# All fourteen later heads' values by seven products, and output product 2 in the attention's last period

## The chip, the core and the metric

The kernel runs on one core of one Trainium2 chip. The metric is the device time of one execution in microseconds (us). Five engines work side by side, each through its own list of instructions in order: PE (TensorE, the matmuls), DVE (VectorE), ACT (ScalarE), POOL (GpSimd) and SP (SyncE, which here issues the transfers).

## The reference, cut to what matters

One block of a streaming encoder on a 512 x 2048 sequence, in float32:

```
h    = rmsnorm(x)
proj = h @ w_in                    # q, k, v of 8 + 8 heads of 128 columns, and 8 forget gates
o_sb  = stick_breaking(qa, ka, va) # 8 heads
o_fox = softmax with a decay by the gates (qf, kf, vf)  # 8 heads
x = x + concat(headnorm(o_sb), headnorm(o_fox)) @ w_out
x = x + relu(rmsnorm(x) @ w_up)**2 @ w_down
y = rmsnorm(x)
```

## The kernel before, in words

**Products in three parts.** Every matrix product is made of pairs: a float32 operand is cast to fp32r (the high part, on ACT) and the rest is the low part (a subtraction, on DVE). `mm3` (L76) multiplies high by high, high by low and low by high into one PSUM bank, so a tile of weights costs a load, a cast, a low part and matmuls in threes.

**Seven products for eight.** The larger products go by Winograd's form of Strassen's scheme: the operands are cut into 2 x 2 quadrants and seven products p = 1 to 7 of quadrants or of their sums replace eight. The sums are made on DVE.

**Stages.** (1) Values (V) of the first two heads and the gates, plain. (2) V of twelve heads in two groups of six by the seven-product scheme: each product is 48 matmuls with 384 columns (`NV`), into one of three PSUM banks x, y and z (two of PSUM's eight rooms each). Group 2 runs its products in the order 2, 1, 5, 6, 4, 7, 3 in banks x, y, z, y, x, y, z. At a product's end `saved` (ACT) and `added` (DVE, L566 to L569) scale the bank's rows into a tile, and SP stores it as `vd`. (3) The attention: sixteen heads in periods of 26.05 us, in which PE makes the next head's q and k (`accq`, 96 matmuls with 512 columns), the scores `s` of one head and the output `o` of another. The pool `accb` for half of the `accq` and for `accv` takes over rooms of the V stage. (4) The last period has no next head; PE fills it with `last_values`: V of the last two heads, plain, 192 matmuls with 256 columns into `accv`, and `take_last_values` splits them. (5) The output projection by seven products (banks `accoa`, `accob`, `accoc`), product 2 first for both halves (db) of the columns; the last two heads' outputs `o` and `oq` and their norms are made in between: `square`, `square_low` (L951: the low part of the squares, in `n` for the head before the last and in `pl` for the last), `norm_sums` (L956 and L957: two matmuls with a matrix of ones) and `norm_2`. (6) MLP up and down by seven products.

**What sets the order.** Up to the end of the attention the order within each engine is written out by hand: `plan.at(time, job)` sorts jobs by a planned time. What comes after it (`g_form`, the left operands `g` of the output's products, made from `mixed`; the weights `wo`, `wh`, `wl`) is placed by a scheduler, which may slip it into the list between the jobs of the plan. An instruction waits until what it reads is there and what it overwrites has been used, and all behind it on its engine wait with it.

Of the kernel before, what the change touches and what calls it, by code (L numbers as in the profile page):

```python
# [15 lines left out]
P = 128  # L16
# [12 lines left out]
NV = 3 * P  # L29

# [7 lines left out]
def block_kernel(ctx, tc, x, g_attn, w_in, b_f, g_out_sb, g_out_fox, w_out, g_mlp, w_up, w_down, g_final, y):  # L38
# [82 lines left out]
    vd = [dp.tile([P, TB, 2 * P], F32, name="vd0")] + [dp.tile([P, TB, 2 * NV], F32, name=f"vd{i}") for i in (1, 2)]  # L121
# [99 lines left out]
    with ExitStack() as stage:  # L221
# [12 lines left out]
        def vtile(i):  # L234
            return vq[min(i, 1)].tile([P, K8, NV], F32, tag=f"q{i}", name=f"q{i}")
# [160 lines left out]
        def load_rows_of(t_, group, name, a, b=None):  # L396
            s, j = int(name[0]) - 1, int(name[1]) - 1
            c0 = v_columns(order[2 if group == 1 else 8]) + j * NV
            b = a if b is None else b
            sp.dma_start(t_[:, b:b + 2], vrows[s][:, a:a + 2, c0:c0 + NV])  # L400

        def load_quadrant(group, name, i, rows=range(0, K8, 2)):
            if rows[0] == 0:
                quads[group][name] = vtile(i)
            for a in rows:
                load_rows_of(quads[group][name], group, name, a)
# [52 lines left out]
        class Product(Piece):  # L459
            def __init__(self, p, group, a, T, first):  # L460
                self.p, self.a0, self.T, self.group = p, a, T, group
                self.a, self.b, self.first = 2, NV, first
                self.names = {1: ("11",), 2: ("21",), 3: ("22",), 5: ("11", "12", "11"), 6: ("11", "22", "11"),
                              4: ("21", "21", "11"), 7: ("12", "22", "12")}[p]

            def source(self):
                if self.p == 1 and self.group == 1:
                    return early_11[self.a0 // 4][:, self.a0 % 4:self.a0 % 4 + 2]
                return quads[self.group][self.names[0]][:, self.a0:self.a0 + 2]

            def sum(self):
                out, u, v = (quads[self.group][n][:, self.a0:self.a0 + 4] for n in self.names)
                dve.tensor_tensor(out, u, v, op=ALU.subtract)
# [8 lines left out]
            def multiply(self):  # L482
                ps = self.T[0]
                for t in range(2):
                    ts = slice(t * P, (t + 1) * P)
                    for i in range(2):
                        k = self.a0 + i
                        lh, ll = self.left(k)
                        mm3(ps[:, t, :NV], lh[:, ts], ll[:, ts], self.hi[:, i, :], self.lo[:, i, :],
# [8 lines left out]
        STARTS[2] = {p: END + i * TP for i, p in enumerate((2, 1, 5, 6, 4, 7, 3))}  # L498
        TE = TV + END + 7 * TP
# [8 lines left out]
        def product(p, group, T, new=None, leads=(6.4, 4.2, 2.6)):  # L508
# [3 lines left out]
            for n, a in enumerate(range(0, K8, 2)):  # L512
                w = Product(p, group, a, T, new is not None)
                tm = t + TP / 4 * n
# [45 lines left out]
        def saved(name, tile_, T, t0):  # L560
            out = keep[name] = tile_()
            for i in range(2):
                act.mul(out[:, i, :], T[0][:, i, :NV], r1s[0][:, t0 + i:t0 + i + 1])

        def added(name, T, t0, group, j):
            out = keep[name]  # L566
            for i in range(2):
                dve.scalar_tensor_tensor(out[:, i, :], T[0][:, i, :NV], r1s[0][:, t0 + i:t0 + i + 1], out[:, i, :], op0=ALU.mult, op1=ALU.add)
            sp.dma_start(vd[group][:, t0:t0 + 2, j * NV:(j + 1) * NV], out)  # L569
# [4 lines left out]
        def gates_0():  # L574
            t_ = vf.tile([P, K8 * 2 * P], F32, tag="e3", name="gt")
            gate["tri"], gate["one"] = t_[:, :P], t_[:, P:2 * P]
            r_ = vf.tile([P, K8 * 2 * P], F32R, tag="e4", name="gr")
# [1597 lines left out]
```

## Time and profile before

| | |
|---|---|
| median of 3 runs | 2005.12 us (2004.80 to 2005.39) |
| profiled execution, its own time | 2005.12 us |
| its span (first to last instruction) | 2003.4 us |
| PE busy | 1993.2 us, 10288 matmuls |
| DVE busy | 1746.6 us |
| ACT busy | 1201.9 us |
| mean granted TensorE clock | 0.999 |

A row of the timeline gives the start, the duration, the engine, the line, the operation, what it writes and reads and, in brackets, how long the engine had stood idle and who released it. Matmuls overlap, so their pace is the distance from start to start and not the duration.

### The profile page before, as it was taken

The numbers are of one execution on the slowest core, as the hardware profiler recorded it, in microseconds if no ns is written. First come the engines' busy times: TensorE is split into PE (matmuls) and PEld (weight loads), VectorE is DVE, ScalarE is ACT, GpSimd is POOL, SyncE is SP. The second block draws the span as 40 slices with busy tenths as digits, with TensorE's granted clock in tenths as the row PEclk, the third lists the DMA queues.
The fourth block names the chain that finished last, engine by engine and source line by source line (L and its number), as shares of the span: only waits on it lengthen the run. The fifth ranks groups of instructions, "written<-read, shape, count | busy, mean of one in ns | idle before, by whom it ended". The sixth has DMA issues, their size and how long they took to land.

```text
span 2003.4 us, 27063 instructions
## 1 busy us (share of the span) xinstructions
PE 1993.2 (99%) x10288; PEld 1726.3 (86%) x10288; DVE 1746.6 (87%) x1993; ACT 1201.9 (60%) x1643; POOL 64.1 (3%) x73
## 2 busy tenths in 40 slices
PE   9999999999999999999999999999999999999998
PEld 9998888888898889888888888888888888888887
DVE  8886888888877588999999999998798888988896
ACT  7544766787764565767676776766543444444344
POOL 0000011010110000000000000000000000000003
PEclk9999999999999999999999999999999999999999
DMA  7417976777658962666666666666695674674642
GB/s 262 157 65 248 291 232 209 228 223 223 207 177 303 304 227 95 199 202 199 217 183 214 199 207 200 200 209 233 246 334 177 226 277 146 239 263 171 214 163 85
DMA packets 309570, 423.54 MB, mean 211 GB/s; under 512 B 49424, under 2 KB 205376, under 8 KB 302912
## 3 DMA queue, kind: packets, MB, share of 16 engines
q1 hardware_dynamic: 308688, 419.71, 63.6%
q10 hardware_dynamic: 752, 2.11, 0.3%
q8 instruction: 81, 1.33, 0.3%
q14 instruction: 49, 0.40, 0.1%
HBM read 315.45 MB, written 96.49 MB: 206 GB/s over the span
## 4 chain that ended last, share of the span: by engine, by line
PE 98%; DVE 1%; DMA 1%; ACT 0%; issue 0%; SPq 0%; DVEq 0%; ACTq 0%
PE psa L1311 11%; PE accd L78 8%; PE accd L79 8%; PE accd L77 8%; PE accq L77 6%; PE accq L78 6%; PE accq L79 6%; PE psa L1309 6%; PE psc L1311 5%; PE psc L1309 3%; PE psb L1311 3%; PE psb L1309 1%; PE m L78 1%; PE m L77 1%; PE m L79 1%; PE accoc L77 1%
## 5 line engine op out<-in xcount | busy, mean ns | idle before, releaser
L1961 ACT CAST wh<-wd 128x1024 fp32r<-128x1024 f32 x126 | 124.9, 998 | 169.7 <-PE accd L79 59.0
L1847 DVE TENSOR_TENSOR wl<-wu,wh 128x1024 fp32r<-128x1024 f32 x158 | 192.7, 1220 | 12.1 <-ACT wh L1841 11.9
L77 PE MATMUL accq<-hH,wh 128*128 128x512 f32 x512 | 200.3, 391 | 0.0
L78 PE MATMUL accq<-hL,wh 128*128 128x512 f32 x512 | 199.4, 389 | 0.0
L79 PE MATMUL accq<-hH,wl 128*128 128x512 f32 x512 | 199.4, 389 | 0.0
L1841 ACT CAST wh<-wu 128x1024 fp32r<-128x1024 f32 x158 | 167.5, 1060 | 44.1 <-issue 27.9
L1311 PE MATMUL psa<-f,wh 128*128 128x512 f32 x720 | 179.0, 391 | 0.0
L78 PE MATMUL accd<-wl,uf 128*128 128x512 f32 x436 | 169.6, 389 | 0.0
L79 PE MATMUL accd<-wh,uf 128*128 128x512 f32 x436 | 169.6, 389 | 0.0
L77 PE MATMUL accd<-wh,uf 128*128 128x512 f32 x436 | 169.4, 389 | 0.0
L1311 PEld LDWEIGHTS psa<-f,wh 128*128 128x128 f32 x720 | 132.3, 188 | 25.6
L1968 DVE TENSOR_TENSOR wl<-wd,wh 128x1024 fp32r<-128x1024 f32 x126 | 144.0, 1152 | 10.6 <-ACT wh L1961 10.6
L1961 ACT CAST wx<-wd 128x1024 fp32r<-128x1024 f32 (+1 forms) x82 | 80.7, 994 | 106.1 <-PE accd L79 39.6
L1682 DVE TENSOR_TENSOR m<-m,accd 128x1024 f32<-128x1024 f32 x84 | 102.3, 1217 | 45.9 <-PE accd L79 45.9
L79 PEld LDWEIGHTS accq<-hH,wl 128*128 128x128 f32 x512 | 96.1, 188 | 20.3
L77 PEld LDWEIGHTS accq<-hH,wh 128*128 128x128 f32 x512 | 96.2, 188 | 19.0
L78 PEld LDWEIGHTS accq<-hL,wh 128*128 128x128 f32 x512 | 96.2, 188 | 18.9
L77 PE MATMUL accd<-wx,uf 128*128 128x512 f32 x284 | 110.5, 389 | 0.0
L78 PE MATMUL accd<-wx,uf 128*128 128x512 f32 x284 | 110.5, 389 | 0.0
L79 PE MATMUL accd<-wx,uf 128*128 128x512 f32 x284 | 110.5, 389 | 0.0
L1309 PEld LDWEIGHTS psa<-f,wl 128*128 128x128 f32 x720 | 96.0, 191 | 5.4
L1309 PE MATMUL psa<-f,wl 128*128 128x256 f32 x720 | 98.3, 282 | 0.0
(464 smaller groups left out, 5121.3 us busy)
## 6 DMA issues: line engine op xcount, KB each, us to landing
wu<-in_w_up_dram SPq DMA_DIRECT2D x60, 1024.0 KB, 6.3
ufd<-st SPq DMA_DIRECT2D x98, 512.0 KB, 4.0
wd<-in_w_down_dram SPq DMA_DIRECT2D x48, 1024.0 KB, 9.2
uf<-ufd SPq DMA_DIRECT2D x42, 1024.0 KB, 8.1
wraw<-in_w_in_dram SPq DMA_DIRECT2D x68, 512.0 KB, 5.7
wo<-wsums SPq DMA_DIRECT2D x28, 512.0 KB, 5.4
q<-in_w_in_dram SPq DMA_DIRECT2D x32, 384.0 KB, 5.5
wd<-in_w_down_dram SPq DMA_DIRECT2D x16, 768.0 KB, 5.8
```

The lines of the kernel that those rows point to most:

```text
L77: pe.matmul(out, sh, mh, start=first, stop=False, skip_group_check=True)
L78: pe.matmul(out, sh, ml, start=False, stop=False, skip_group_check=True)
L79: return pe.matmul(out, sl, mh, start=False, stop=last, skip_group_check=True)
L1309: ins = pe.matmul(ps[:, 2 * P:], lo[:, a, :], f_parts(p, a)[0], start=False, stop=last, skip_group_check=True)
L1311: ins = pe.matmul(ps, hi[:, a, :], f_both(p, a), start=a == PAIRS[0] and p in (1, 5), stop=last, skip_group_check=True)
L1682: dve.tensor_tensor(M[p][:, :, db, :], M[p][:, :, db, :], ps, op=ALU.add)
L1841: act.copy(rooms[k][0], srcs[k])
L1847: lows[0] = dve.tensor_tensor(lo, srcs.pop(k), hi.bitcast(F32), op=ALU.subtract)
L1961: act.copy(rooms[k + 3][0], srcs[k + 3])
L1968: dve.tensor_tensor(rooms[k + 2][1], srcs.pop(k + 2), rooms[k + 2][0].bitcast(F32), op=ALU.subtract)
```

## The change

Group 2 now holds all eight remaining heads: its products have 512 columns (`NVS[2]`), 48 matmuls each, and the plan gives each of them 10.9 us (`TP2`) for 8.45. The quadrants no longer fit where they were, so tiles are cut in 6 + 2 rows (`load_late`, `quad`), quadrant 21 is loaded twice (`21x`), and sums over a second half are made in two pieces. The order of the products becomes 2, 1, 5, 6, 3, 7, 4, so that the last is product 4 in bank x. The gates' jobs move to 33.0 to 48.5 us in the group. `last_values` and `take_last_values` are gone.

The attention's last period is filled with the output's product 2 (classes `FoxLeft` and `Second`): 96 matmuls with 512 columns into four tiles `acc2`, of which `take_second` adds the results to rows of x. The output stage then begins with product 1; product 4 of the first half follows early, in bank b.

```diff
-        STARTS[2] = {p: END + i * TP for i, p in enumerate((2, 1, 5, 6, 4, 7, 3))}
+        TP2 = 10.9
+        STARTS[2] = {p: END + i * TP2 for i, p in enumerate((2, 1, 5, 6, 3, 7, 4))}
...
             def sum(self):
-                out, u, v = (quads[self.group][n][:, self.a0:self.a0 + 4] for n in self.names)
-                dve.tensor_tensor(out, u, v, op=ALU.subtract)
+                for a, n in ((self.a0, 4),) if self.group == 1 or self.a0 == 0 else ((4, 2), (6, 2)):
+                    out, u, v = (quad(self.group, name, a, n) for name in self.names)
+                    dve.tensor_tensor(out, u, v, op=ALU.subtract)
...
-                pieces = []
-                for a in range(4):
-                    c = v_columns(order[2 * NH - 2])
-                    k0 = 4 * a
-                    w = Piece(w_in[k0 * P:(k0 + 4) * P, c:c + 2 * P].rearrange("(a p) c -> p a c", p=P), 4, 2 * P)
-                    cast, low = ((-9.25, -3.65), (2.3, 3.3), (3.3, 4.5), (10.25, 11.7))[a]
-                    pieces.append(w.plan(plan, t + (-21.0, -15.0, -14.0, -2.0)[a], t + cast, t + low))
+                for i, jobs in ((1, (-9.25, -3.65)), (0, (2.3, 3.3))):
+                    for dt, f in zip(jobs, (fox_left.high, fox_left.low)):
+                        plan.at(t + dt, f, i)
...
+                        for tt in range(2):
+                            plan.at(t + at_unit16(unit), w.multiply, tt)
+                            unit += 1
+                for db in range(2):
+                    plan.at(t + 2.0 + db, load_second_x, db)
+                    for tt in range(2):
+                        plan.at(t + (20.6, 28.5)[db] + 0.75 * tt, take_second, db, tt)
+                t_end = t + at_unit16(15) + 1.37
...
-        for i, dt in ((2 * NH - 2, 1.0), (2 * NH - 1, 3.0)):
+        t = TPER * 2 * NH
+        for i, times in ((2 * NH - 2, (at_unit16(14) - 1.95, 23.1, 24.9, at_unit16(15) + 1.37, 27.4, 29.0)),
+                         (2 * NH - 1, (28.5, 30.5, 32.2, 33.0, 33.5, 34.8))):
             H = heads[i]
-            plan.at(t_end + dt, H.product)
-            plan.at(t_end + dt + 2.0, H.square)
-            plan.at(t_end + dt + 3.7, H.square_low)
-            plan.at(t_end + dt + 4.5, H.norm_sums)
-            plan.at(t_end + dt + 5.0, H.norm_1)
-            plan.at(t_end + dt + 6.3, H.norm_2)
+            for dt, f in zip(times, (H.product, H.square, H.square_low, H.norm_sums, H.norm_1, H.norm_2)):
+                plan.at(t + dt, f)
...
-            g_form(2, (0, 4), (4, 8))
             g_form(1, (0, 4), (4, 6))
             with tc.issue_after(last_heads[2].ins):
                 g_form(4, (0, 4), (4, 8))
                 g_form(5, (0, 4), (4, 6))
...
             with tc.issue_after(last_heads[3].ins):
-                out_piece(2, 0, 2)
+                out_piece(1, 0, 0)
+            with tc.issue_after(last_heads[0].ins):
+                out_piece(1, 0, 2)
+                out_piece(1, 0, 4)
+            begin(1, 0, 0)
+            with tc.issue_after(last_heads[1].ins):
+                for m0 in (0, 2, 4, 6):
+                    ins = out_piece(4, 0, m0)
...
-        for p in G_ORDER:
+        for p in (1, 5, 6, 3, 7, 4)[:6 if db else 5]:
```

In the rows below, what an instruction waits for stands in brackets, by engine or transfer queue.

**From the values to the attention, PE.** Before, the last matmuls of the V stage (bank z) and the first of the attention stand so:

```order
L77 MATMUL vz_1350<-wh_1700,s3_1000 128x384
L78 MATMUL vz_1350<-wl_1701,s3_1000 128x384
L79 MATMUL vz_1350<-wh_1700,s3_1000 128x384
L77 MATMUL accq_1773<-hH0_98,wh_1716 128x512 [waits Activation_49]
L78 MATMUL accq_1773<-hL0_99,wh_1716 128x512
```

and now (bank x) so:

```order
L78 MATMUL vx_1682<-wh_1719,hH3_104 128x512
L79 MATMUL vx_1682<-wl_1720,hH3_104 128x512
L80 MATMUL vx_1682<-wh_1719,hL3_105 128x512
L78 MATMUL accq_1793<-hH0_98,wh_1735 128x512 [waits DVE_49,Activation_49]
L79 MATMUL accq_1793<-hL0_99,wh_1735 128x512
```

The first matmul of the attention waited for ACT's cast alone and now waits for DVE too: its tile lies in rooms of bank x, and DVE's last `added` reads `vx_1682`.

**The same place, SP.** `s0_1525` is the tile of the last `added` before, `s3_1700` that of the change; `wraw` are raw weights of the first head's k (two halves) and of the next head's q. Before:

```order
L569 DMA vd2_89<-s2_1681 128x2x384 [waits DMAHW3_49,DVE_49]
L733 DMA rb_1763<-r1d_91 128x512 [waits DMAHW4_49,DMAHW6_49,DMAHW0_49,PE_49]
L165 DMA wraw_1765<-in_w_in_dram 128x8x128 [waits DMAHW5_49]
L165 DMA wraw_1767<-in_w_in_dram 128x8x128 [waits DMAHW3_49]
L569 DMA vd2_89<-s0_1525 128x2x384 [waits DMAHW7_49,DVE_49]
L165 DMA wraw_1769<-in_w_in_dram 128x8x128 [waits DMAHW1_49,Activation_49]
```

and now:

```order
L590 DMA vd2_89<-gt_1444 128x2x512 [waits DMAHW7_49,DVE_49]
L590 DMA vd2_89<-s3_1700 128x2x512 [waits DMAHW0_49,DVE_49]
L783 DMA rb_1783<-r1d_91 128x512 [waits DMAHW3_49,DMAHW1_49,PE_49]
L166 DMA wraw_1785<-in_w_in_dram 128x8x128 [waits DMAHW2_49]
L166 DMA wraw_1787<-in_w_in_dram 128x8x128
L166 DMA wraw_1789<-in_w_in_dram 128x8x128 [waits DMAHW6_49,DMAHW4_49,Activation_49]
```

The last store stood behind `rb` and two loads of weights; now all three stand behind it.

**The end of the attention, DVE.** `p_last` is the low part of the last head's weights, made when its transposes are done; `pl` in the last row is that head's `square_low`. Before (a row with x2 stands for two instructions):

```order
L913 TENSOR_TENSOR p_last_5466<-pt_5443,p_last_5466 128x1280 [waits DMAHW1_49,Activation_49]
L63 SCALAR_TENSOR_TENSOR vl_5482<-accv_5220,r1v_147,vh_5481 128x256 [waits Activation_49] x2
L63 SCALAR_TENSOR_TENSOR vl_5482<-accv_5221,r1v_147,vh_5481 128x256 [waits Activation_49] x2
L60 TENSOR_TENSOR g4_5576<-mixed_1750,g4_5575 128x1024 x2
L60 TENSOR_TENSOR wx_5687<-wo_5688,wx_5687 128x1024 [waits DMAHW7_49,DMAHW5_49,DMAHW0_49]
L60 TENSOR_TENSOR wl_5705<-wo_5706,wh_5704 128x1024 [waits DMAHW6_49,DMAHW2_49,Activation_49]
L1231 TENSOR_TENSOR mixed_1750<-mixed_1750 128x4x256 [waits DVE_49]
L1231 TENSOR_TENSOR mixed_1750<-mixed_1750 128x2x256 [waits DVE_49]
L951 TENSOR_TENSOR n2_5510<-n1_5509,n2_5510 128x512 [waits Activation_49]
L951 TENSOR_TENSOR pl_5531<-ph_5530,pl_5531 128x512 [waits PE_49,Activation_49]
```

In the change the head before the last has its `n2` ahead of `p_last`, and eight instructions follow `p_last` in these rows:

```order
L962 TENSOR_TENSOR p_last_5462<-pt_5443,p_last_5461 128x1280 [waits Activation_49]
L1167 TENSOR_TENSOR x2_5289<-x2_5289,acc2_5361 128x512 [waits DMAHW2_49]
L61 TENSOR_TENSOR g4_5526<-mixed_1770,g4_5525 128x1024 x2
L61 TENSOR_TENSOR wl_5620<-wo_5621,wh_5619 128x1024 [waits DMAHW6_49,Activation_49]
L1332 TENSOR_TENSOR mixed_1770<-mixed_1770 128x4x256 [waits DVE_49]
L61 TENSOR_TENSOR wl_5638<-wo_5639,wh_5637 128x1024 [waits DMAHW1_49,DMAHW2_49,DMAHW0_49,Activation_49]
L1332 TENSOR_TENSOR mixed_1770<-mixed_1770 128x2x256 [waits DVE_49]
L1015 SCALAR_TENSOR_TENSOR n1_5438<-ssq_5465,ra_5437 128x512 [waits Activation_49]
```

The next ten and the last head's `square_low` follow directly:

```order
L61 TENSOR_TENSOR g5_5520<-mixed_1770,g5_5519 128x1024 [waits PE_49,Activation_49]
L61 TENSOR_TENSOR wl_5656<-wo_5657,wh_5655 128x1024 [waits DMAHW3_49,DMAHW2_49,Activation_49]
L1016 TENSOR_TENSOR n1_5438<-n1_5438,ra_5437 128x512 [waits DVE_49]
L61 TENSOR_TENSOR g5_5520<-mixed_1770,g5_5519 128x512 [waits Activation_49]
L1334 TENSOR_TENSOR mixed_1770<-mixed_1770 128x4x256 [waits DVE_49]
L61 TENSOR_TENSOR wx_5673<-wo_5674,wx_5673 128x1024 [waits DMAHW5_49,DMAHW4_49,Activation_49]
L1017 SCALAR_TENSOR_TENSOR n1_5438<-n1_5438,ra_5437 128x512 [waits DVE_49]
L1334 TENSOR_TENSOR mixed_1770<-mixed_1770 128x2x256 [waits DVE_49]
L1018 SCALAR_TENSOR_TENSOR mixed_1770<-os_5436,g_rest_78,n1_5438 128x512 [waits DVE_49]
L1167 TENSOR_TENSOR x2_5289<-x2_5289,acc2_5362 128x512
L1000 TENSOR_TENSOR pl_5492<-ph_5491,pl_5492 128x512
```

The `g5` lows, the whole `norm_2` of the head before the last and two of the lows of weights stood behind `pl` before, the rows of x (`x2`) not at all in this place; now 18 instructions stand between `p_last` and `pl`, nine of 1024 elements a row and nine of 512.

**The same place, PE.** The matmuls that end with the last head's norm sums, in the change (the 24 `accoa` matmuls between the `oq` product and them end with the first two rows):

```order
L79 MATMUL accoa_5549<-wx_5602,g1_5515 128x512
L80 MATMUL accoa_5549<-wx_5602,g1_5516 128x512
L1005 MATMUL oq_5471<-pl_5492,onesr_114 128x512 [waits Activation_49]
L1006 MATMUL oq_5471<-pl_5492,onesr_114 128x512 [waits DVE_49]
L78 MATMUL accob_5550<-wh_5619,g4_5525 128x512
L79 MATMUL accob_5550<-wl_5620,g4_5525 128x512
```

From the last transpose to the first of the two norm sums PE's list holds 19 matmuls with 512 columns, one sum for the head before the last, the 12 of `oq` and 24 of `accoa`.

More of the change, by code (lines that the diff above doesn't have):

```diff
@@ L672, in block_kernel @@
             X4 = [None]
-            product(2, group, T["x"], "x", (6.9, 4.3, 2.4))
-            plan.at(TV + 13.5 if one else at_[1] + 0.6, saved, "11", lambda: stored(0), T["x"], 0)
+            product(2, group, T["x"], "x", (0, 4.3, 2.4))
+            plan.at(TV + 13.5 if one else at_[1] + 0.6, saved, "11", (lambda: stored(0)) if one else (lambda: third(NVS[2])), T["x"], 0)
             product(1, group, T["y"], "y")
```

258 lines of the change are left out of this document (157 added, 101 removed).

## Prediction

> **What bounds the kernel now.** I read the page's first and fourth parts, then windows around the places that the change touches.
>
> ```profile
> span 2003.4 us, 27063 instructions
> ...
> PE 1993.2 (99%) x10288; PEld 1726.3 (86%) x10288; DVE 1746.6 (87%) x1993; ACT 1201.9 (60%) x1643; POOL 64.1 (3%) x73
> ...
> PE 98%; DVE 1%; DMA 1%; ACT 0%; issue 0%; SPq 0%; DVEq 0%; ACTq 0%
> ```
>
> PE is idle for 10.2 us of 2003.4 and the chain of waits is 98% PE. So the time moves in two ways: by fewer matmul columns, and by every wait that PE newly takes. The windows (V group 2, the start of the attention, its last period, the output) show how little slack for a gain there is:
>
> ```profile
> core 0: us, PE busy (x) PEld busy (x) DVE busy (x) ACT busy (x) POOL busy (x), PEclk, DMA share, GB/s
> 117.00:165.00 48.00, 48.00 (x280) 48.00 (x279) 38.08 (x46) 22.54 (x35) 0.68 (x4) 1.00 0.14 45
> 165.00:190.00 25.00, 25.00 (x115) 20.89 (x114) 14.49 (x20) 8.36 (x11) 1.80 (x2) 1.00 0.94 315
> 560.00:600.00 40.00, 40.00 (x287) 37.88 (x286) 28.90 (x34) 28.64 (x31) 3.77 (x6) 1.00 0.55 176
> 600.00:646.00 46.00, 46.00 (x209) 38.19 (x208) 37.61 (x48) 21.23 (x36) 0.00 (x0) 1.00 0.85 297
> 646.00:650.00 4.00, 3.22 (x13) 2.11 (x12) 2.38 (x2) 2.02 (x3) 0.00 (x0) 1.00 1.03 375
> ```
>
> PE is busy for the whole of the first four windows: both places where the change cuts in, the seam from the values to the attention and the attention's end, have no PE wait today. Only the output stage has one, near 647.
>
> **Matmuls.** Matmuls overlap, so their price is the distance between starts.
>
> ```profile
> 156.76 0.33 PE L77 MATMUL vz<-wh,s 128*128 128x384 f32 x1
> ...
> 165.08 0.39 PE L77 MATMUL accq<-hH,wh 128*128 128x512 f32 x1
> ...
> 563.50 0.28 PE L77 MATMUL accv<-wh,hH 128*128 128x256 f32 x1
> 563.61 0.28 PE L78 MATMUL accv<-wl,hH 128*128 128x256 f32 x1
> 563.73 0.28 PE L79 MATMUL accv<-wh,hL 128*128 128x256 f32 x1
> ...
> 605.15 0.39 PE L77 MATMUL accob<-wx,g 128*128 128x512 f32 x1
> ...
> 616.03 0.39 PE L77 MATMUL accoc<-wx,g 128*128 128x512 f32 x1
> ```
>
> ```profile
> L77 PE MATMUL accv<-wh,hH x64: 277/283/364, 563.5 to 591.8; 128*128 128x256 f32 x64
> ```
>
> A V product's 48 matmuls of 384 columns take 165.08 - 156.76 = 8.32 us, 0.1733 each. A product's half in the output, 48 of 512 columns, takes 616.03 - 605.15 = 10.88 us, 0.2267 each. 256 columns take 0.12. The change drops 3 x 64 = 192 of 256 columns (-23.0 us) and widens 7 x 48 = 336 matmuls from 384 to 512 columns, 336 x 0.0534 = +17.9 us. Output product 2's 96 matmuls are moved, not added. Sum: **-5.1 us**.
>
> **The seam.** The first `accq` now waits for the last `added`, because bank x, in whose room it is made, is read last.
>
> ```profile
> 165.28 1.14 DVE L568 SCALAR_TENSOR_TENSOR s<-vz,r1v,s 128x384 f32<-128x384 f32 x2 [1.81 <-PE vz L79]
> ...
> 168.20 1.23 DVE L179 TENSOR_TENSOR wl<-wraw,wh 128x1024 fp32r<-128x1024 f32 x1 [1.78 <-ACT wh L172]
> 169.35 0.68 DVE L741 SCALAR_TENSOR_TENSOR qf<-accq,rb 128x512 f32<-128x512 f32 x1
> ```
>
> ```profile
> 167.12 1.05 ACT L172 CAST wh<-wraw 128x1024 fp32r<-128x1024 f32 x1 [4.90 <-DMA wraw<-in_w_in_dram]
> ...
> 172.39 1.05 ACT L172 CAST wh<-wraw 128x1024 fp32r<-128x1024 f32 x1 [1.71 <-DMA wraw<-in_w_in_dram]
> ```
>
> ```profile
> 160.59 0.99 SPq L733 DMA_DIRECT2D rb<-r1d  x1
> 161.63 1.69 SPq L165 DMA_DIRECT2D wraw<-in_w_in_dram  x2
> 166.45 0.37 SPq L569 DMA_DIRECT2D vd<-s  x1
> 166.92 0.42 SPq L165 DMA_DIRECT2D wraw<-in_w_in_dram  x1
> ```
>
> Let S be the moment at which the last V matmul gives way to the next. Before, `added` began 0.20 us after it. Two of 512 columns at 0.68, with some 0.08 of overlap, end at S + 1.48; with a hop to PE the `accq` starts at S + 1.5. Behind that `added` SP's queue holds the store, then `rb`, then the second half of the first k's weights. Before, those weights were asked for at 161.63, ahead of the last store; now the store is issued at S + 1.5, `rb` 0.47 us later (166.45 to 166.92) and the weights 1.04 after that (160.59 to 161.63): S + 3.0. From issue to the start of the cast it took 5.49 us (161.63 to 167.12) and 5.47 (166.92 to 172.39), so the cast runs from S + 8.5 to S + 9.55. PE has 24 matmuls to do with the first half, 5.44 us, and is done at S + 6.95: a wait of 2.6 us. The third matmul wants the low part, 1.23 us after the cast, less the two matmuls before it: 0.8 more. Together 1.5 + 2.6 + 0.8 = **+4.9 us**. Ends: 1.5 if the weights land before S + 6 (then nothing is added to the first wait), 6.5 if the queue, with more to move at 315 GB/s, is a good us slower.
>
> **Inside group 2.** A product has 10.9 us for four lows of 1024 elements, a sum of 2048 and two to four takes.
>
> ```profile
> L473 DVE TENSOR_TENSOR q<-q,q 128x1536 f32<-128x1536 f32 x8 | 14.0, 1752 | 0.0
> ```
>
> Estimate for 2048 elements from 1.75 (1536) and 1.23 (1024): 2.3 us. 4 x 1.23 + 2.3 + 4 x 0.68 = 9.9 of 10.9 us: it fits. In product 6 one low part stands behind such a sum and the gates' small steps: 0 to 1.1 us, I take **+0.6**. The loads of quadrants have whole products of time and cost nothing; if one is late it is a cast that waits.
>
> **The end of the attention.** This is the largest term.
>
> ```profile
> 588.20 1.25 PE L885 MATMUL pt<-ident,w 128*128 128x128 f32 x10
> ...
> 596.82 0.44 PE L77 MATMUL oq<-p_last,vh 128*128 128x512 f32 x1
> ...
> 598.74 0.44 PE L77 MATMUL accoa<-wh,g 128*128 128x512 f32 x1
> ...
> 604.70 0.39 PE L956 MATMUL oq<-pl,onesr 128*128 128x512 f32 x1
> ```
>
> ```profile
> 590.75 1.49 DVE L913 TENSOR_TENSOR p_last<-pt,p_last 128x1280 fp32r<-128x1280 f32 x1 [3.92 <-ACT p_last L910]
> ...
> 595.00 2.35 DVE L60 TENSOR_TENSOR g<-mixed,g 128x1024 fp32r<-128x1024 f32 x2
> ...
> 601.28 0.68 DVE L951 TENSOR_TENSOR n<-n,n 128x512 fp32r<-128x512 f32 x1
> 601.88 0.68 DVE L951 TENSOR_TENSOR pl<-ph,pl 128x512 fp32r<-128x512 f32 x1
> ```
>
> Let R be the end of the last transposes (589.45 before). `pl` was done at 602.56, 2.1 us ahead of the sum that needs it. In the change 18 DVE instructions stand between `p_last` and `pl`. `p_last` starts at R + 1.30 and leaves DVE to the next at R + 2.7. In a row, 1024 elements cost 2.35 - 1.22 = 1.13 us and 512 cost 0.60 (601.28 to 601.88): 9 x 1.13 + 9 x 0.60 = 15.6, so `pl` runs from R + 18.3 to R + 19.0. PE's list to the sum of `pl` is 45 matmuls of 512 columns at 0.2267 (10.2 us) and the `oq` product, 598.74 - 596.82 = 1.92: R + 12.1. PE then stands for **+7.0 us**, and all of the output stage with it. A shorter way to the same place bounds it below: the cast for the low part of `wx_5673`, five rows above `pl`, overwrites a room that the last `accoa` matmul before the sums still reads (R + 11.9); cast 1.05, low 1.13, four small ones and `pl` 3.1 give R + 17.2, a wait of 5.1. Without any overlap between instructions it is 8.5.
>
> **The clock.** Seven idle us are longer than any wait in the trace of before after its start. At the start PE ran slowly:
>
> ```profile
> 1.58 1.65 PE L305 MATMUL vx<-still 128*128 128x256 f32 x6 [1.58 <-DVE still L301]
> ...
> 3.37 0.58 PE L305 MATMUL vx<-still 128*128 128x256 f32 x1
> ```
>
> (1.65 - 0.58) / 5 = 0.214 us per matmul of 256 columns, against 0.12 later: a rate of 0.56. If PE falls back to that for as long as it took then, some 2 to 4 us, it loses 0.9 to 1.8 us; if not, nothing. I take the middle, **+0.9**. The Trainium skill ("TensorE: Matmul & The Clock Gate", Part 1: The HAM clock gate) says that one idle window of about 3.4 us halves the clock and about 3.4 us of work restores it: by that this term would be 1.7 and the sum 0.8 higher. Before's trace has no such wait, so it neither confirms nor denies it.
>
> **The rest.** `acc2`'s later weights are loaded in the period itself, behind transfers that wait for rooms: 0 to 2 us, I take **+0.5**. In the output stage before has one wait, for a low part:
>
> ```profile
> 647.03 0.50 PE L77 MATMUL accoa<-wh,g 128*128 128x512 f32 x1
> 648.29 0.50 PE L78 MATMUL accoa<-wl,g 128*128 128x512 f32 x1 [0.76 <-DVE wl L60]
> ```
>
> It costs 1.26 - 0.23 = 1.0 us. The new order of products may lose it, or put one in its place where two quarters are turned in a row: 0, with 1.0 either way. The attention's full periods and the MLP are not touched.
>
> **Sum.** -5.1 + 4.9 + 0.6 + 7.0 + 0.9 + 0.5 = +8.8 us. The profiled execution took 2005.12 us, which is also the median of the three runs, 1.7 us beyond its span; so 2013.9 us. A difference under 0.2%, 4.0 us, can't be told from no change here.
>
> **Rivals.**
>
> 1. *The seam is short.* The weights land in time, since SP's wait falls in a calm stretch, and only the 1.5 us for the bank are left: 8.8 - 3.4 = +5.4, 2010.5. For it speaks the window of group 2 (45 GB/s); against it two latencies of 5.5 us that agree. Chance 0.17.
> 2. *Everything that waits for transfers is late, and the clock falls.* Seam 6.0, `acc2` 2.0, clock 1.8: -5.1 + 6.0 + 0.6 + 7.0 + 2.0 + 1.8 = +12.3, 2017.4. For it: the stretch after the seam moves 315 GB/s and the `acc2` loads share the queue with the output's. 0.23.
> 3. *The costs just cancel the gain.* Seam 1.5, the tail at its lower end 5.1, nothing else but 0.3: +1.8, 2006.9. 0.09.
> 4. *Faster: PE never waits at the end.* Then the matmuls decide. Place: DVE's 18 instructions between `p_last` and `pl`. It needs them done within PE's 9.3 us after `p_last` hands over, 0.5 us each for 0.87 by the rows; the point is where tail and seam together stay under 5.1 us. With a seam of 1.5: -5.1 + 1.5 + 0.6 = -3.0, and with 0.0 inside group 2 and the wait at 647 gone -4.6: about 2001. Against it: the list is fixed, and the rows agree on these durations wherever they stand. 0.06.
>
> My forecast has 0.45, its own range 2010 to 2018. The change does what it says: its list has no `accv` left, 96 `acc2` matmuls and 336 V matmuls of 512 columns.
>
> **Range.** Outside 2008.0 to 2018.5 lie rival 4, most of rival 3 and the upper part of rival 2, together about 0.2. Slower by over 0.2%: forecast, 1 and 2, 0.85; within: rival 3, 0.09; faster: 0.06.
>
> **What would show it.** In the profile of after: V group 2 about 76 us long; a DVE `added` ending the idle time of the first `accq`, then a cast of `wraw` ending a second one 5.4 us later; near the end of the attention one PE wait of 5 to 8 us that ends at a low part `pl`; a row of matmuls behind it at 0.4 us and more if the clock fell. I am wrong if PE has no wait over 3 us there, or if the seam shows only the wait for the bank.

## The result and the profile after

| | before | after |
|---|---|---|
| median | 2005.26 us (2004.80 to 2006.23, 4 runs) | 2017.67 us (2017.34 to 2020.62, 4 runs) |
| profiled execution, its own time | 2005.12 us | 2017.39 us |
| its span | 2003.4 us | 2015.7 us |

The changed kernel is slower: ratio 1.0065, 95% interval 1.0047 to 1.0082, or 12.4 us between the medians and 12.3 between the spans. First the page of after:

```profile
span 2015.7 us, 26681 instructions
...
PE 1993.9 (99%) x10096; PEld 1711.7 (85%) x10096; DVE 1754.7 (87%) x1992; ACT 1203.8 (60%) x1636; POOL 65.6 (3%) x73
...
PE 95%; DVE 2%; DMA 1%; ACT 1%; issue 0%; SPq 0%; POOL 0%; DVEq 0%; ACTq 0%; POOLq 0%
```

The 192 matmuls are gone (10288 to 10096), yet PE's share of the chain of waits fell from 98% to 95%. The chain now passes through DVE, ACT and a transfer where PE stands. PE's busy time did not fall with them, in part because a matmul that runs at a lower clock is busy for longer. PE's waits by releaser show where it stands (us in total, times, the longest):

```profile
PE oq L1006 <- DVE pl L1000: 7.0, 1, 7.0
PE accq L78 <- ACT wh L173: 2.5, 1, 2.5
PE accq L78 <- DVE s L588: 1.6, 1, 1.6
PE vx L306 <- DVE still L302: 1.6, 1, 1.6
```

The fourth row is the kernel's start and stood in before too. The rest are new: one long wait at the attention's end and two at the seam from the values to the attention; no other is over 0.6 us. The windows of after cover group 2, the seam, and the long wait with what follows it:

```profile
core 0: us, PE busy (x) PEld busy (x) DVE busy (x) ACT busy (x) POOL busy (x), PEclk, DMA share, GB/s
107.00:184.00 77.00, 76.46 (x341) 63.17 (x340) 57.56 (x58) 34.04 (x42) 0.68 (x4) 1.00 0.33 113
184.00:200.00 16.00, 11.40 (x48) 8.51 (x47) 5.72 (x7) 3.67 (x4) 0.00 (x0) 1.00 0.78 242
...
626.00:640.00 14.00, 7.03 (x24) 5.30 (x23) 12.63 (x20) 4.09 (x7) 0.00 (x0) 0.76 0.35 100
```

In the last row PE works for half of the window, DVE nearly all of it, and the granted clock is 0.76. That is the only one of these windows below 1.00.

**The seam.** The timeline of after, PE first, then DVE, ACT and SP's queue:

```profile
184.84 0.39 PE L80 MATMUL vx<-wh,hL 128*128 128x512 f32 x1
186.82 0.47 PE L78 MATMUL accq<-hH,wh 128*128 128x512 f32 x1 [1.59 <-DVE s L588]
...
192.16 0.39 PE L80 MATMUL accq<-hH,wl 128*128 128x512 f32 x1
195.02 0.50 PE L78 MATMUL accq<-hH,wh 128*128 128x512 f32 x1 [2.48 <-ACT wh L173]
...
196.28 0.50 PE L80 MATMUL accq<-hH,wl 128*128 128x512 f32 x1 [0.53 <-DVE wl L180]
196.62 0.39 PE L78 MATMUL accq<-hH,wh 128*128 128x512 f32 x1
...
185.26 1.41 DVE L588 SCALAR_TENSOR_TENSOR s<-vx,r1v,s 128x512 f32<-128x512 f32 x2 [3.08 <-PE vx L80]
...
193.93 1.04 ACT L173 CAST wh<-wraw 128x1024 fp32r<-128x1024 f32 x1 [13.00 <-DMA wraw<-in_w_in_dram]
...
186.70 0.36 SPq L590 DMA_DIRECT2D vd<-s  x1
187.16 0.41 SPq L783 DMA_DIRECT2D rb<-r1d  x1
187.62 4.51 SPq L166 DMA_DIRECT2D wraw<-in_w_in_dram  x3
```

From 184.84 to 196.62 there are 28 steps, 28 x 0.2267 = 6.35 us at the usual pace; they took 11.78. The seam costs 5.4 us. SP asks for the weights only at 187.62, behind the last store, which itself waits for `added`; the cast of them starts 6.3 us later. The first of the three loads at 187.62 is the second half of the first head's k; the other two are halves of the next head's q, since the first half of k was asked for in group 2 already, at 165.37.

**The end of the attention.** The timeline of after again, PE and then DVE:

```profile
626.56 0.39 PE L1005 MATMUL oq<-pl,onesr 128*128 128x512 f32 x1
633.91 0.79 PE L1006 MATMUL oq<-pl,onesr 128*128 128x512 f32 x1 [6.97 <-DVE pl L1000]
634.51 0.63 PE L78 MATMUL accob<-wh,g 128*128 128x512 f32 x1
634.93 0.63 PE L79 MATMUL accob<-wl,g 128*128 128x512 f32 x1
...
638.17 0.40 PE L78 MATMUL accob<-wh,g 128*128 128x512 f32 x1
...
616.09 1.49 DVE L962 TENSOR_TENSOR p_last<-pt,p_last 128x1280 fp32r<-128x1280 f32 x1 [1.47 <-ACT p_last L959]
...
633.18 0.68 DVE L1000 TENSOR_TENSOR pl<-ph,pl 128x512 fp32r<-128x512 f32 x1
```

DVE is busy without a break from `p_last` to `pl`, and PE's second norm sum waits for it: 633.91 - 626.56 - 0.23 = 7.1 us. Behind the wait the matmuls start 0.43 us apart and not 0.23, as the second and third row behind it show: ten steps from 633.91 to 638.17 take 4.26 us where 2.27 is usual, 2.0 us more.

**The start.** One microsecond of the difference is none of the change's doing. The first matmul of the first `accq` in the V stage, ahead of anything that the change moves on PE, in before, in after, and in an experiment told below (the banks' order alone):

```profile
62.10 0.39 PE L77 MATMUL accq<-hH,wh 128*128 128x512 f32 x1
```

```profile
63.26 0.39 PE L78 MATMUL accq<-hH,wh 128*128 128x512 f32 x1
```

```profile
61.58 0.39 PE L78 MATMUL accq<-hH,wh 128*128 128x512 f32 x1
```

Over all fourteen profiled executions it lies between 61.58 and 63.36.

### The profile page after: what moved, and what is told of

It reads as the page before. It is cut to its first block, busy times and chain, and to the rows that moved or that the text cites. A ratio compares the mean times of both kernels' runs of the same rounds, so it can differ in the third digit from the quotient of the medians.

```text
span 2015.7 us, 26681 instructions
## 1 busy us (share of the span) xinstructions
PE 1993.9 (99%) x10096; PEld 1711.7 (85%) x10096; DVE 1754.7 (87%) x1992; ACT 1203.8 (60%) x1636; POOL 65.6 (3%) x73
## 4 chain that ended last, share of the span: by engine, by line
PE 95%; DVE 2%; DMA 1%; ACT 1%; issue 0%; SPq 0%; POOL 0%; DVEq 0%; ACTq 0%; POOLq 0%
PE psa L1412 11%; PE accd L80 8%; PE accd L78 8%; PE accd L79 8%; PE psa L1410 6%; PE accq L78 6%; PE accq L80 6%; PE accq L79 6%; PE psc L1412 5%; PE psc L1410 3%; PE psb L1412 3%; PE psb L1410 1%; PE m L78 1%; PE m L80 1%; PE m L79 1%; PE vy L79 1%
## 5 line engine op out<-in xcount | busy, mean ns | idle before, releaser
L2053 DVE TENSOR_TENSOR wl<-wd,wh 128x1024 fp32r<-128x1024 f32 x126 | 143.8, 1151 | 12.3 <-ACT wh L2046 12.3
```

The costliest lines, as they stand in the source:

```text
L2053: dve.tensor_tensor(rooms[k + 2][1], srcs.pop(k + 2), rooms[k + 2][0].bitcast(F32), op=ALU.subtract)
```

## The experiments

Every kernel below is after with an edit. Each was compared with before on the same chip, and the times are medians. Where a time is set against after's 2017.67 us, the two come from different sessions, in which before's median lay between 2005.26 and 2006.11. My theory: the 12 us are waits for instructions that stand late in DVE's and SP's lists, and a slow stretch of PE behind each long gap. The rivals: a mended list only uncovers the next late one, and the slow stretch is no matter of idle time.

**1. The last head's norm earlier.** Its squares and their low part are planned ahead of `norm_2` of the head before.

```diff
-                         (2 * NH - 1, (28.5, 30.5, 32.2, 33.0, 33.5, 34.8))):
+                         (2 * NH - 1, (28.5, 28.52, 28.54, 33.0, 33.5, 34.8))):
```

> One line is moved: the last head's square and square_low stand in the plan ahead of the norm of the head before it, so the low part pl follows p_last after seven DVE instructions instead of eighteen. Theory (the tail wait is DVE's list and nothing else, and the slow matmuls behind it come from that wait): the 7.0 us wait of the norm sums goes, and with it the pace of 0.43 us per matmul for about 9 matmuls (1.9 us): 2017.6 - 8.9 = about 2008.7 us. Rival (the DVE work is only moved, and the output stage waits for it a little later, at product 1's last piece or at product 5): at most 3 us come back, 2014.5 us or more, with a new PE wait of several us between 626 and 665.

Measured: 2020.43 us (2019.23 to 2021.51), before 2005.78, ratio 1.0073 (1.0061 to 1.0086). The theory's number failed. `pl` is done at 626.1 now and the norm sums run on time, but the very next matmul stands:

```profile
635.06 0.79 PE L78 MATMUL accob<-wh,g 128*128 128x512 f32 x1 [6.87 <-DVE x L1167]
```

`accob` overwrites rooms of `acc2`, which `take_second` (L1167) still has to read, and that instruction stands at the end of the same list, at 634.33. The gap is the same 6.9 us; only its name changed. Behind it the slow stretch is longer than in after (14 steps from 635.06 to 641.08, 2.8 us lost for 2.0), and waits of 0.4, 0.5 and 0.8 us follow up to 674, which goes some way to the 2.8 us by which this kernel is slower than after.

**2. PE kept busy in the wait.** 30 matmuls of 512 columns that nobody reads, into a free part of the `oq` tile, between the last head's two norm sums. They add work, and the DVE list is as in after.

```diff
-                    self.o, self.q = oq[:, :NT], oq[:, NT:2 * NT]
+                    self.o, self.q, self.idle = oq[:, :NT], oq[:, NT:2 * NT], oq[:, 2 * NT:]
...
-                pe.matmul(self.q, onesr, self.sh, start=True, stop=False)
-                last_heads[1] = pe.matmul(self.q, onesr, self.sl, start=False, stop=True)
+                pe.matmul(self.q, onesr, self.sh, start=True, stop=False, skip_group_check=True)
+                if self.i == 2 * NH - 1:
+                    for _ in range(30):
+                        pe.matmul(self.idle, onesr, self.sh, start=True, stop=True, skip_group_check=True)
+                last_heads[1] = pe.matmul(self.q, onesr, self.sl, start=False, stop=True, skip_group_check=True)
```

> 30 extra matmuls of 512 columns, into a part of a PSUM tile that nothing reads, stand between the two norm sums of the last head; 30 x 0.227 = 6.8 us, so they fill the wait of 7.0 us and add nothing of use. Theory (the idle time lowers the clock, and the slow pace behind it is that): the granted clock stays at 1.00 between 626 and 640, the matmuls of accob run at 0.227 from the first, and the time falls by 1.9 us to about 2015.7 us though there are more matmuls. Rival (the slow pace comes from operands or weights of accob that arrive late): the pace behind the wait stays at 0.43 and the time at 2017.6 us or a little more.

Measured: 2015.59 us (2015.04 to 2017.35), ratio 1.0051 (1.0039 to 1.0064), 2.1 us under after with 30 more matmuls.

```profile
633.90 0.50 PE L1009 MATMUL oq<-pl,onesr 128*128 128x512 f32 x1 [0.17 <-DVE pl L1000]
634.24 0.40 PE L78 MATMUL accob<-wh,g 128*128 128x512 f32 x1
634.48 0.39 PE L79 MATMUL accob<-wl,g 128*128 128x512 f32 x1
```

The second norm sum starts at 633.90 as in after (633.91), but behind it the pace is 0.23 from the second matmul on. It is the idling that slows PE, and at this place that costs 2 us.

**3. The first k's second half of weights asked for ahead of the last store**, into a buffer of its own.

```diff
+        first_pieces.append(q_piece(0, 1, 1))
+        plan.at(TV + END2 - 2.0, first_pieces[3].load)
...
-                        cast, low, load = 16.3, 18.2, 0.3
+                        pieces.append(first_pieces[3].plan(plan, None, t + 16.3, t + 18.2))
+                        continue
```

> The second half of the first head's k weights is asked for ahead of the last store of values, in the last product of group 2, and not behind it. Theory (the second wait at the seam is SP's queue, in which the load stands behind the store that waits for DVE): the waits of 2.6 us (for the cast) and 0.7 us (for its low part) go, the 1.75 us for the bank stay: 2017.6 - 3.4 = about 2014.2 us. Rival (the load is late because the transfers themselves are slow there, whoever is first): the wait moves by less than 1 us and the time stays above 2016.5 us.

Measured: 2015.82 us (2014.02 to 2017.00), ratio 1.0050 (1.0036 to 1.0064). The seam's second and third waits are gone; the first, 1.6 us, stays. In the attention's first `o` stands a new one:

```profile
235.09 0.39 PE L79 MATMUL o<-pl,vh 128*128 128x256 f32 x1 [1.14 <-DVE pl L957]
```

It waits for a low part and takes back over 1 us of the 3 that the queue gave.

**4. The seam's first `accq` in another bank's room.** The V banks are laid out in the order z, x, y, so that the room of the bank that is read last is not the one that `accq` needs first.

```diff
-        vps = [stage.enter_context(tc.tile_pool(name=f"v{c}", bufs=1, space=PSUM, reuse_waits="tile")) for c in "xyz"]
+        vps = [stage.enter_context(tc.tile_pool(name=f"v{c}", bufs=1, space=PSUM, reuse_waits="tile")) for c in "zxy"]
...
-            return vps["xyz".index(c)].tile([P, 2, NT], F32, tag=c, name=f"v{c}")
+            return vps["zxy".index(c)].tile([P, 2, NT], F32, tag=c, name=f"v{c}")
```

> The three banks of the V stage change places, so that accb takes the rooms of bank z, whose last product is the fifth, and the first accq no longer waits for the last added; the queue of transfers is as in the change. Theory (the two waits of the seam are one chain: the weights are issued behind the store, and come when they come): the first wait of 1.75 us goes and the second grows by the same, time unchanged, 2017.6 us within 0.6. Rival (the waits add up independently): 1.75 us are saved, 2015.9 us.

Measured: 2020.11 us (2018.87 to 2021.52), ratio 1.0073 (1.0060 to 1.0086), some 2 us over after.

```profile
188.60 0.39 PE L80 MATMUL accq<-hH,wl 128*128 128x512 f32 x1
193.79 0.79 PE L78 MATMUL accq<-hH,wh 128*128 128x512 f32 x1 [4.80 <-ACT wh L173]
...
199.48 0.58 PE L78 MATMUL accq<-hH,wh 128*128 128x512 f32 x1
```

The waits are one chain, as predicted: without the first, the second grew from 2.5 to 4.8 us. What my expectation missed is the clock. In after's profile two gaps with 24 matmuls between them left it alone; here one gap of 5.2 us from start to start has matmuls of 0.43 us behind it up to 199.48, for 5.7 us. So taking a wait away gained nothing (the ranges of this kernel and of after overlap). That the merging of the gaps cost the clock is not shown: in the profiles of experiments 5 and 9 the seam is after's, with both gaps, and the clock fell there too. In experiment 5 the row at which it shows is:

```profile
195.18 0.79 PE L80 MATMUL accq<-hH,wl 128*128 128x512 f32 x1 [0.53 <-DVE wl L180]
```

From there to 198.33 its matmuls start 0.43 us apart.

**5. The rooms of `acc2` freed earlier as well.** Experiment 1, and `take_second` of the last half ahead of the lists that delayed it.

```diff
-                        plan.at(t + (20.6, 28.5)[db] + 0.75 * tt, take_second, db, tt)
+                        plan.at(t + (20.6, 28.4)[db] + (0.75, 0.01)[db] * tt, take_second, db, tt)
```

> As e_tail, and the second half's two additions of acc2 to x (take_second) stand directly behind p_last as well, so that both things PE needs from DVE there, pl and the freeing of acc2's room for accob, come within 8 and 2 instructions of p_last. Theory (two PE needs stood behind the same list; e_tail freed one and left the other): p_last hands over at R + 2.7, pl is done at R + 10.9 and PE needs it at R + 12.1, so no wait over 0.5 us between 616 and 645 and a granted clock of 1.00 there; 2017.6 - 7.0 - 2.0 = about 2008.6 us. Rival (DVE's work is only put off): a wait of over 2 us shows up again behind 645, time above 2011.

Measured: 2017.23 us (2015.58 to 2018.50), before 2005.32, ratio 1.0057 (1.0045 to 1.0070). The rival was right. The waits for `pl` and for the rooms are gone, and PE's next long one, with DVE's rows ahead of what ends it, is:

```profile
660.10 1.97 PE L1556 MATMUL tr<-ident,x 128*128 128x128 f32 x8 [4.98 <-DVE x L1549]
...
656.50 2.42 DVE L1336 TENSOR_TENSOR mixed<-mixed 128x1024 f32<-128x1024 f32 x3
658.84 1.21 DVE L1549 TENSOR_TENSOR x<-x,accoa 128x1024 f32<-128x1024 f32 x1
```

The transposes of x wait for its sum, which stands behind sums of `mixed` in DVE's list. The wait has moved by 26 us and shrunk from 7.0 to 5.0.

**6. Both mends of the seam (3 and 4).**

> The edits of e_queue and e_bank together: the weights are asked for ahead of the last store, and accb lies in bank z's rooms. Theory (each of the two causes the whole wait if the other is left, since the weights' issue hangs on the last added; together they remove it): no PE wait over 0.3 us between 183 and 200, 2017.6 - 5.2 = about 2012.4 us, up to 1.5 more if the first o product waits for DVE as in e_queue. Rival (the bank edit costs time by itself, as its time of 2020.1 could be read): 2015 us or more.

Measured: 2015.79 us (2014.96 to 2017.65), ratio 1.0053 (1.0040 to 1.0066). Neither wait at the head of `accq` is left, but low parts come late behind them: 1.2 us in `accq`, 1.1 in the first scores (for a cast `uk` on ACT), 0.9 in the first `o`. Of the 5.4 us that the seam costs, 1.9 came back by the medians. The time is in the rival's range, but its reason (the bank edit costs time by itself) is not shown: what the profile shows is the next late jobs.

**7. The seam (3, 4) and the tail (5) together.**

> The edits of e_tail2 and e_seam together. Theory (the waits are independent of each other, and without them the change keeps its 5 us of matmuls): 2017.6 - 9.0 - 5.2 = about 2003.4 us, below the kernel before. Rival (what is gained at one place is given back by work that DVE and the transfers then have to do in less time): over 2007 us.

Measured: 2012.83 us (2012.14 to 2014.81), ratio 1.0038 (1.0025 to 1.0050), where 2003.4 was expected. The transposes' wait is 4.4 us here too. A window over the end of the attention and the output's start:

```profile
616.00:660.00 44.00, 39.58 (x177) 32.91 (x176) 41.19 (x53) 22.46 (x34) 0.00 (x0) 0.96 0.74 262
```

DVE works for 41.19 of 44 us, PE for 39.58. In before's window of 46 us at this place PE was busy for all of it and DVE for 37.61. That leaves a new order little to gain there, though the edits of experiments 9 and 10 together still gain 3.6 us over experiment 8.

**8. And the gates two microseconds later**, with the sum ahead of product 7 nearer to it, so that group 2's low part is not late.

```diff
-        for dt, f in ((33.0, gates_0), (36.5, gates_1), (37.5, gates_2), (43.5, gates_3), (45.0, gates_4), (47.0, gates_5), (48.5, gates_6)):
+        for dt, f in ((33.0, gates_0), (38.5, gates_1), (39.5, gates_2), (45.5, gates_3), (47.0, gates_4), (49.0, gates_5), (50.5, gates_6)):
...
-                product(7, group, T["y"], leads=(19.0, 4.5, 2.9))
+                product(7, group, T["y"], leads=(16.5, 4.5, 2.9))
```

> As e_all, and in group 2 the gates' steps (but the first) stand 2.0 us later and product 7's first sum 2.5 us later, so that product 6's last low part stands ahead of them on DVE. Theory: the wait of 0.7 us near 148 goes, about 0.8 us less than e_all: 2002.6. Rival (the gates then come too late for the attention, or another low part waits): no gain over e_all.

Measured: 2012.17 us (2010.90 to 2013.30), ratio 1.0033 (1.0021 to 1.0045). The 0.5 us wait in group 2 is gone; the median moved by 0.7, within the two ranges.

**9. The sums of `mixed` held back** until after the addition for which the transposes wait (the seam left as it is in after).

```diff
-                dve.tensor_tensor(quarter[q][:, t, :], quarter[q][:, t, :], ps[:, t, :], op=ALU.add)
+                last_heads[4] = dve.tensor_tensor(quarter[q][:, t, :], quarter[q][:, t, :], ps[:, t, :], op=ALU.add)
...
-            last_heads[4] = lows[0]
```

> As e_tail2, and DVE's sums for products 3 and 7 (4.8 us in e_all, needed only from product 3 on) are placed behind the addition of product 1 to x, for which the transposes waited 5.0 us in e_tail2. Theory (DVE's list, not its total work, decides which of PE's needs comes late; the wait moved from pl to accob to the transposes because each time something that is not urgent stood ahead): no wait over 2 us between 616 and 720; the 5.0 us and the slow pace behind them (about 2.2 us) go, about 1.6 us come back where product 3 then waits for a cast: 2017.2 - 7.2 + 1.6 = about 2011.6 us. Rival (DVE is short of time as such in the first 45 us of the output stage): a wait of 4 us or more shows up behind 650, time 2015 us or more.

Measured: 2016.09 us (2011.34 to 2017.35), before 2006.11, ratio 1.0047 (1.0033 to 1.0061). The transposes no longer wait, and the next matmuls do, for the output's weights: first for a cast, then for a load from memory.

```profile
657.68 0.50 PE L78 MATMUL accoc<-wh,g 128*128 128x512 f32 x1 [1.18 <-ACT wh L60]
661.13 0.80 PE L78 MATMUL accoa<-wh,g 128*128 128x512 f32 x1 [2.94 <-DMA wh<-whigh]
```

The median is the rival's (2015 or more), but its wait of 4 us is not there: the longest is 2.9. The five executions differ by the clock: four with a mean granted clock of 0.996 or 0.997 took 2015.51 us or more, and the one at 0.999 took 2011.34, near the 2011.6 of the theory. The profile is of one of the four; its clock fell twice, at the seam and behind the wait at 661.

**10. All that helped, with the last store on ACT's queue** and no longer ahead of `rb` and the weights on SP's: 4, 5, 8, 9 and this.

```diff
-            sp.dma_start(vd[group][:, t0:t0 + 2, j * n:(j + 1) * n], out)
+            (act if (name, group) == ("21", 2) else sp).dma_start(vd[group][:, t0:t0 + 2, j * n:(j + 1) * n], out)
```

> The edits of e_best and e_tail3, but the last store of values of group 2 is issued by ACT and not by SP, so that both rb and all three loads of weights are free of the wait for DVE (e_best frees one load, and DVE waits 5.2 us for rb). Theory (all that is late is late because of what stands ahead of it in a list): at the seam no PE wait over 0.3 us up to 230, at the tail as e_tail3: 2012.2 - 5.3 + 1.6 - 3.0 = about 2005.5 us, the time of the kernel before. Rival (the 5 us of matmuls are paid back in waits wherever the list is mended): 2010 us or more.

Measured: 2008.56 us (2006.84 to 2011.26, 11 runs), before 2006.11 (15 runs), ratio 1.0014 (1.0005 to 1.0022). The seam has no wait left and this is the best of the mended versions, but it is still slower than before: the median lies between the theory's 2005.5 and the rival's 2010. The profile is of the slowest of the 11 executions, 2011.26 us. In the output's start two windows of this kernel, and its transfers there (KB each, median us from issue to landing), show what is late now:

```profile
646.00:652.00 6.00, 5.23 (x27) 3.80 (x25) 6.00 (x8) 3.90 (x8) 0.00 (x0) 1.00 1.03 391
652.00:658.00 6.00, 2.74 (x6) 2.00 (x7) 6.00 (x8) 3.50 (x7) 0.00 (x0) 0.73 0.99 381
```

```profile
wl<-wsums SPq DMA_DIRECT2D x3, 512.0 KB, 8.9
...
wx<-wsums SPq DMA_DIRECT2D x1, 512.0 KB, 9.6
```

DVE is busy all the time, the DMA engines are too, and PE waits 1.4 and 2.6 us and then runs slowly (clock 0.73).

**11 and 12. Cover given back.** What all these mends share is the place: the output's start, from which the change took output product 2, 96 x 0.2267 = 21.8 us of PE's work. If that was the cover under which DVE and the transfers got ready, then useless matmuls there should cost nothing up to the length of the waits. Experiment 10 with the lines of experiment 2, with 30 and with 96 matmuls:

> The kernel with all the mended lists (2008.56 us) plus 30 matmuls of 512 columns that nobody needs, between the last head's two norm sums at 622. They take 30 x 0.2267 = 6.8 us of PE and give the lists behind it 6.8 us more before PE reaches its next needs. Theory (the output's start lacks cover for the work that is queued on DVE and in the transfers there): the two waits near 653 (1.4 and 2.6 us) and the slow matmuls behind them (655.8 to 661.5, some 2.7 us lost) go, 6.7 us in all, so that the 30 matmuls cost next to nothing: 2008.6, within 2007 to 2010.5, and the profile shows no wait over 1 us between 640 and 670. Rival (those waits hang on rooms that PE itself frees, so they move along with it): the waits stay and the time is 2008.6 + 6.8 = 2015.4.

> The same with 96 such matmuls, 21.8 us, as many as output product 2 has, which stood at the output's start before the change. Theory: cover beyond what the waits took is plain loss, so 2008.6 + 21.8 - 6.7 = 2023.7, no wait over 1 us and no slow matmuls between 650 and 690. Rival: 2030.4.

Measured: 2010.54 us (2008.61 to 2013.94, 7 runs), before 2005.55, ratio 1.0026 (1.0014 to 1.0037), and 2023.51 us (2022.59 to 2024.48), ratio 1.0087 (1.0072 to 1.0102). With 30:

```profile
621.91 6.96 PE L1008 MATMUL oq<-pl,onesr 128*128 128x512 f32 x30
...
660.76 0.50 PE L79 MATMUL accoa<-wx,g 128*128 128x512 f32 x1 [0.62 <-DMA wx<-wsums]
```

```profile
640.00:670.00 30.00, 29.38 (x133) 24.03 (x133) 20.44 (x24) 13.47 (x21) 0.00 (x0) 1.00 0.87 297
```

Of 6.8 us of useless work 4.8 came back by the medians (2010.54 - 2008.56 = 2.0), 4.4 by the ratios (0.0012 x 2005 = 2.4), and the only wait between 640 and 700 is 0.6 us, at full clock. The rival (waits on rooms that PE itself frees, so that they move along with it) asked for 2015.4. The time lies just above what the theory allowed (2010.5). That less than 6.7 us came back may be because the waits and the slow stretch had been read from experiment 10's slowest execution. The other 66 matmuls, 66 x 0.2267 = 15.0 us, cost 13.0, most of their length, since no long wait was left to fill. So the lack of cover is shown: the mended lists moved the wait and shortened it, and none of them removed it; more work for PE at this place did.

## Why the prediction was right in direction and too low by 3.8 us

The terms of the sum against the profiled execution of after:

| step | predicted | measured | from |
|---|---|---|---|
| matmuls | -5.1 | -5.1 | by count, 192 fewer and 0.2267 for 512 columns; not measured apart |
| seam | +4.9 | +5.4 | 28 steps in 11.78 us |
| inside group 2 | +0.6 | +0.9 | the rows below |
| tail | +7.0 | +7.1 | 633.91 - 626.56 - 0.23 |
| clock | +0.9 | +2.0 | ten steps in 4.26 us |
| `acc2` loads, output | +0.5, 0 | +0.8 | what is left of 12.3 |
| start | not in the sum | +1.2 | 63.26 - 62.10 |
| sum | +8.8 | +12.3 | spans |

Group 2 runs from its first matmul, below, to the first row of the seam, 184.84 + 0.23; the second row is its longest wait:

```profile
107.55 0.39 PE L78 MATMUL vx<-wh,hH 128*128 128x512 f32 x1
...
149.32 0.50 PE L79 MATMUL vy<-wl,s 128*128 128x512 f32 x1 [0.54 <-DVE wl L180]
```

That is 77.5 us for 336 x 0.2267 = 76.2, or 1.3 more. Before's group 2 took 58.7 us (106.40 to 165.08) for 336 x 0.1733 = 58.2, so 0.4 of the 1.3 stood there before, and the change added 0.9.

**The matmuls and the cover.** Right as far as it can be told: by count they save 5.1 us, and nothing else in the change saves any.

**The seam.** The mechanism was right in its order and in each releaser: `added`, the cast, the low part. Two sizes were off and nearly cancel: `rb` held SP's queue for 0.46 us (187.16 to 187.62) where I took 1.04, and from issue to cast it took 6.3 us where two rows of before had said 5.5. The half microsecond that is left stands at the heads of the gaps: the first wait cost 1.75 us for 1.5. Rivals 1 and 3 (the seam is short) fell; experiment 4 shows that the waits are one chain and experiment 3 that the second and third were the queue's.

**The tail.** Right to 0.1 us: 18 instructions of DVE in a row, priced by before's rows. Rival 4 (PE never waits at the end) fell with it. The prediction's reason was incomplete in one way: it read `pl` as the cause. Experiments 1, 5, 9 and 10 showed that four needs of PE stood late together (`pl`, `acc2`'s rooms, the sum for the transposes, the weights), and 11 that, with the lists mended, 6.8 us of other PE work at this place removes what is left of the waits but for 0.6 us.

**The clock.** This is the step that was mis-sized: "I take the middle, +0.9". The stretch behind the wait lost 2.0 us, and experiment 2 shows that idling is the cause. I had taken a middle between nothing and 1.8 from the start's matmuls; the upper end was right. The estimate of 1.7 by the Trainium skill ("TensorE: Matmul & The Clock Gate", Part 1: The HAM clock gate) was nearer. The pace that it gives for the slow state, 426.7 ns for 512 columns, is the 0.43 of the rows above.

**Rival 2** named 2017.4, close to the median, but for reasons that hold only in part: the clock fell as it said and the seam's weights came late, though `acc2`'s did not cost 2 us. What it lacked was made up by group 2, the start and what is left over, so that its sum of 12.3 is the measured one by luck.

**Left open.** The 4 runs of after spread over 3.3 us, those of before over 1.4. The clock differs between executions too: the mean granted clock of after was 0.998 in the profiled one and 0.996 in the other three, as low as in experiment 4 (0.995 and 0.996). So the other three probably lost more by the clock than the +2.0 of the table, which holds for the profiled execution alone; where, no profile shows.

## What to carry to other kernels

Work moved out of a place takes its cover with it: before moving a product away, ask what DVE and the transfers made ready underneath it, and compare their busy time in that window with what PE will have left. Price an idle gap of PE at the gap plus what a fall of the clock may add: 1.6 to 2.8 us where it was read here. Every wait of 4.0 us or more in these profiles had such a fall, and some of the waits from 1.4 to 2.8 us did. And when a mended wait comes back under another name at nearly the same length, the limit may be the sum of the work and not the list: test it with useless work that fills the gap.

## What the hardware showed that was not expected

**The slow stretch can begin late and without a long gap.** In experiment 9's seam the wait was 2.75 us, the next matmuls ran at full pace for 2.3 us (but for the low part's 0.5), and only then came a slow stretch, the longer durations between the last two rows:

```profile
193.94 0.50 PE L78 MATMUL accq<-hH,wh 128*128 128x512 f32 x1 [2.75 <-ACT wh L173]
...
196.24 0.59 PE L78 MATMUL accq<-hH,wh 128*128 128x512 f32 x1
...
199.61 0.43 PE L80 MATMUL accq<-hH,wl 128*128 128x512 f32 x1
```

It lasted 3.4 us, 196.24 to 199.61. After's seam, with a wait of 2.48 us and the same short one behind it, shows none; experiment 5's, with waits of 2.42 and 0.53 us, does. The shortest wait with a fall behind it is in experiment 8's first scores:

```profile
225.94 0.50 PE L78 MATMUL s<-uk,uh 128*128 128x512 f32 x1 [1.47 <-ACT uk L802]
```

Another 0.22 us of idle follows, and the granted clock between 227 and 230 is 0.50.

The granted clock in the traces of after and of the experiments has, behind the start, 14 spells at 0.50: five last 3.4 us, eight 6.8 and one (experiment 1's) 10.2. Part of a spell can lie inside the wait, where it costs nothing: in after the clock is 1.00 up to 631.1 and 0.50 from there to 637.7, and PE starts again only at 633.91. The Trainium skill (the same page and section) tells of a free-running window of about 3.4 us. The length and the changing onset fit that, but its condition of one idle window of that length does not: here 2.75 us of idle in one piece was enough, and 1.47 with 0.22 behind it. In experiment 4 the slow stretch lasted 5.7 us, in experiment 1 6.0. As a matmul at 0.43 loses 0.20 of it, the price of these gaps is 1.6 us (3.4) to 2.8 us (6.0), by where the spell falls.

**The start varies.** The slow matmuls of the first 10 us put the first `accq` anywhere between 61.58 and 63.36 us, 1.8 us, which is more than many of the differences above; only medians over several executions tell them.

**Loads of 512 KB took 8.9 and 9.6 us** from issue to landing where the core moved 381 to 391 GB/s (experiment 10). Whether an earlier issue of them would have helped was not tried.
